# Mean of ReLU over rows of 1024: the order in which 128 partitions take their runs of rows

## The chip, the cores and the metric

The kernel runs on one core of one Trainium2 chip. The metric is the device time of one execution in microseconds (us). Three runs of the kernel before gave a median of 161.53 us (161.38 to 161.6). A difference of about 0.2% (0.3 us) can be told from none.

## The reference

The input `x` is 32 x 512 x 1024 in float32, 67.1 MB. Each output element is the mean of the positive part of one row of 1024:

```python
def reference(x: np.ndarray) -> np.ndarray:
    relu_x = np.maximum(x, 0)
    return np.mean(relu_x, axis=-1).astype(np.float32)
```

So there are 16,384 rows, each is read once, and 64 KB go out. Rows don't depend on each other: any partition may take any rows, as long as its results go back to the right places.

## The kernel before, in words

**Rows and partitions.** The first 128 rows (`xfirst`) go one to each partition, into `row0`. The other 16,256 rows (`xmain`) are cut into 128 runs of J = 127 neighbouring rows; in the kernel before, partition p takes run p. The view `xr` has the indices (partition, row in the run, column), and `outr` is the same for the output.

**Loads.** All of them are issued by the SP engine in program order and go through one queue. `load` (line 109) issues one transfer and gives it a semaphore of its own. There are seven big loads, each of NB = 16 rows of every run, so 64 KB of neighbouring bytes per partition and 8 MB in all, into three buffers that are used in turn. The tail of each run comes in pieces that get smaller: 7, 4, 2 and 1 rows, and the last row in columns 512, 256 and 256 wide. The function `issue_ahead_of_entry_barrier` moves the first two loads (`row0` and the first big one) ahead of the program's entry barrier. Before the load of a buffer that was used before, `buf_free` (line 115) makes SP wait until both compute engines are done with it. Because SP runs ahead as far as the three buffers let it, there are two or more loads in the queue through most of the program.

**Compute.** Rows with an even number in the run are summed on ScalarE (`act_row`, line 15: ReLU with a running sum) and the odd ones on VectorE (`dve_row`, line 20: max with 0, and a sum). Both wait for the load's semaphore. Sums go to `sums`, one column per row of the run. GpSimd (`finish`, line 157) scales them by 1/1024 into `res`. The row before the last is shared between the two engines by columns, and the last row is summed in three parts. The instruction at line 197 does the last part.

**Stores.** The 128 means of `row0` are stored early, between the big loads (line 125). The other 16,256 means are stored by one transfer from `res` (line 205) after the last sum. SP waits for it, and the program ends.

**What sets the order.** Nothing but the order of the instructions on each engine and the semaphores; there is no planner. [...]

Of the kernel before, what the change touches and what calls it, by code (L numbers as in the profile page):

```python
# [45 lines left out]
def kernel(  # L46
# [11 lines left out]
    P = nc.NUM_PARTITIONS  # L58
# [3 lines left out]
    J = R // P  # L62
    inv = 1.0 / D

    xfirst, xmain = xf[:P, :], xf[P:, :]
    outfirst, outmain = out.flatten()[:P], out.flatten()[P:]
    J = J - 1
    xr = xmain.rearrange("(p j) d -> p j d", p=P, j=J)
    outr = outmain.rearrange("(p j) -> p j", p=P, j=J)

    NB = 16
    BUFS = 3
# [7 lines left out]
    def sbuf(name, *shape):  # L80
        return ctx.enter_context(nc.sbuf_tensor(name, list(shape), F32))

    bufs = [sbuf(f"rows{b}", P, NB, D) for b in range(BUFS)]
# [3 lines left out]
    last = sbuf("last", P, D + 2)  # L87
# [20 lines left out]
    def load(i, dst, src):  # L108
        nc.sync.dma_start(out=dst, in_=src).then_inc(loaded[i], 16)

    def buf_free(t):

        if t >= BUFS:
            nc.sync.wait_ge(act, t - BUFS + 1)
            nc.sync.wait_ge(dve, t - BUFS + 1)

    for t in range(full):
        buf_free(t)
        if t == 0:
            load(-1, row0[:, :], xfirst)  # L120
        load(t, bufs[t % BUFS][:, :, :], xr[:, t * NB:(t + 1) * NB, :])
        if t == BUFS:

            nc.sync.wait_ge(first, 2)
            nc.sync.dma_start(
                out=outfirst.rearrange("(q i) -> q i", i=32), in_=turned0[0:P:32, :],
            ).then_inc(stored, 16)
    j0 = full * NB
    buf_free(full)
    xt = bufs[full % BUFS]  # L130
    lo, i = 0, full
    for n in row_pieces:
        load(i, xt[:, lo:lo + n, :], xr[:, j0 + lo:j0 + lo + n, :])
        lo, i = lo + n, i + 1
    c = 0
    for w in col_pieces:
        load(i, last[:, c:c + w], xr[:, J - 1, c:c + w])
        c, i = c + w, i + 1


# [31 lines left out]
    lo, i = 0, full  # L172
    for n in row_pieces[:-1]:
        rows(i, xt, lo, n, j0)
        lo, i = lo + n, i + 1
# [72 lines left out]
```

## Time and profile before

| what | value |
|---|---|
| median of three runs | 161.53 us |
| the profiled execution's own time | 161.59 us |
| its span, first to last instruction | 160.2 us |
| what lies around the span (161.59 - 160.2) | 1.39 us |
| VectorE busy | 73.3 us (46%) |
| ScalarE busy | 70.4 us (44%) |
| DMA packets' time, as a share of 16 engines' span | 97.7% |
| bytes read from HBM | 67.11 MB |
| mean rate over the span | 419 GB/s |

The span starts with the first instruction and ends with the last one. Busy times of different engines overlap. A DMA packet here is what one DMA engine moves in one piece: for a big load, the 64 KB of one partition. SPq in the profile is SP's sequencer, which issues transfers.

### The profile page before, as it was taken

To read this page: it belongs to the slowest core of one execution; us is meant where nothing else is said; L and a number is where in the kernel's file an instruction comes from. 1 tells how busy PE (TensorE), PEld (TensorE's weight loads), DVE (VectorE), ACT (ScalarE), POOL (GpSimd) and SP (SyncE) were. 2 spreads that over 40 slices of the span, in tenths; PEclk is the share of its full clock that TensorE was granted. 3 is DMA by queue.
4 is the path that set the end of the run, shared out by engine and by line. 5 is a ranking of instruction groups with operands and counts; after the bars stand their busy time and mean duration, and the time that the engine had idled before them with its cause. 6 is when DMAs were issued, how large, how long until landed. Compare 5 with 4: busy or idle time off the path is not lost. (4 is left out here: it accounts for less than half of the span.)

```text
span 160.2 us, 347 instructions
## 1 busy us (share of the span) xinstructions
DVE 73.3 (46%) x131; ACT 70.4 (44%) x133; POOL 1.3 (1%) x9
## 2 busy tenths in 40 slices
DVE  0000029900498006960079500993009920299984
ACT  1400029800496006950079300991009900299983
POOL 1000000000000000000000000000000000000001
DMA  9969969979989899699699699699699797998992
GB/s 393 507 278 523 507 278 523 442 344 523 409 376 523 360 425 524 294 491 523 262 524 523 262 523 524 262 523 523 262 524 458 327 523 327 425 451 367 419 412 102
DMA packets 2312, 67.18 MB, mean 419 GB/s; under 512 B 392, under 2 KB 648, under 8 KB 1032
## 3 DMA queue, kind: packets, MB, share of 16 engines
q1 hardware_dynamic: 2312, 67.18, 97.7%
HBM read 67.11 MB, written 0.07 MB: 419 GB/s over the span
## 5 line engine op out<-in xcount | busy, mean ns | idle before, releaser
L20 DVE TENSOR_SCALAR_CACHE_REDUCE rows<-rows 128x1024 f32<-128x1024 f32 (+1 forms) x63 | 72.1, 1208 | 78.9 <-DMA rows<-in_x_dram 78.7
L15 ACT ACTIVATE rows<-rows 128x1024 f32<-128x1024 f32 x64 | 66.2, 1035 | 84.1 <-DMA rows<-in_x_dram 83.9
L15 ACT ACTIVATION_READ_ACCUMULATOR rows<-rows 128x1 f32 x64 | 11.9, 186 | 0.0
L20 DVE DVE_READ_ACCUMULATOR rows<-rows 128x1 f32 x63 | 5.2, 82 | 0.0
L168 DVE STREAM_TRANSPOSE turned<-mean 128x32 f32<-128x32 f32 x1 | 0.2, 213 | 5.9 <-ACT row L164 5.9
L164 ACT ACT_TABLE_LOAD x1 | 1.3, 1283 | 3.3 <-DMA row<-in_x_dram 3.3
L157 POOL TENSOR_SCALAR res<-sums 128x112 f32<-128x112 f32 (+1 forms) x2 | 0.5, 250 | 154.0 <-DVE rows L20 154.0
L164 ACT ACTIVATE row<-row 128x1024 f32<-128x1024 f32 x1 | 1.1, 1056 | 0.0
L15 ACT ACTIVATE last<-last 128x512 f32<-128x512 f32 x1 | 0.6, 630 | 0.0
L20 DVE TENSOR_SCALAR_CACHE_REDUCE last<-last 128x256 f32<-128x256 f32 x1 | 0.4, 420 | 0.3 <-DMA last<-in_x_dram 0.3
L197 DVE SCALAR_TENSOR_TENSOR last<-last,scale 128x258 f32<-128x258 f32 x1 | 0.4, 428 | 0.1
L142 POOL MEMSET scale<- 128x258 f32 x1 | 0.3, 314 | 0.0
L187 POOL TENSOR_SCALAR res<-part 128x1 f32<-128x1 f32 x1 | 0.3, 267 | 0.6 <-DVE rows L20 0.6
L164 ACT ACTIVATION_READ_ACCUMULATOR row<-row 128x1 f32 x1 | 0.2, 186 | 0.0
L15 ACT ACTIVATION_READ_ACCUMULATOR last<-last 128x1 f32 x1 | 0.2, 186 | 0.0
L141 POOL MEMSET mean<- 128x32 f32 x1 | 0.1, 126 | 1.5 <-POOLq L55 1.5
L232 POOL MEMSET const-uint8-127<- 128x1 uint8 x1 | 0.1, 103 | 0.0
L232 POOL MEMSET const-bfloat16-1.0<- 128x1 bf16 x1 | 0.1, 102 | 0.0
L232 POOL MEMSET const-float32-0.0<- 128x1 f32 x1 | 0.1, 99 | 0.2 <-issue 0.2
L232 POOL MEMSET const-float32-1.0<- 128x1 f32 x1 | 0.1, 99 | 0.0
L20 DVE DVE_READ_ACCUMULATOR last<-last 128x1 f32 x1 | 0.1, 83 | 0.0
L197 DVE DVE_READ_ACCUMULATOR last<-last,scale 128x1 f32 x1 | 0.1, 82 | 0.0
## 6 DMA issues: line engine op xcount, KB each, us to landing
rows<-in_x_dram SPq DMA_DIRECT2D x1, 3584.0 KB, 38.1
rows<-in_x_dram SPq DMA_DIRECT2D x1, 2048.0 KB, 42.6
rows<-in_x_dram SPq DMA_DIRECT2D x1, 1024.0 KB, 44.7
row<-in_x_dram SPq DMA_DIRECT2D x1, 512.0 KB, 3.3
rows<-in_x_dram SPq DMA_DIRECT2D x1, 512.0 KB, 45.4
last<-in_x_dram SPq DMA_DIRECT2D x1, 256.0 KB, 45.6
last<-in_x_dram SPq DMA_DIRECT2D x2, 128.0 KB, 45.4
rows<-in_x_dram SPq DMA_DIRECT2D x7, 48.8
```

The lines of the kernel that those rows point to most:

```text
L15: return nc.scalar.activation(out=src, in_=src, func=ACT.Relu, accum_out=acc)
L20: return nc.vector.tensor_scalar(out=src, in0=src, scalar1=0.0, scalar2=init, op0=ALU.max, op1=ALU.add, accum_out=acc,)
L141: nc.gpsimd.memset(mean0[:, :], 0.0)
L142: nc.gpsimd.memset(scale[:, :], inv).then_inc(pool, 1)
L157: nc.gpsimd.tensor_scalar(out=res[:, lo:hi], in0=sums[:, lo:hi], scalar1=inv, scalar2=0.0, op0=ALU.mult, op1=ALU.add,)
L164: nc.scalar.activation(out=row0[:, :], in_=row0[:, :], func=ACT.Relu, scale=inv, accum_out=mean0[:, 0:1],).then_inc(first, 1)
L168: nc.vector.transpose(turned0[:, :], mean0[:, :]).then_inc(first, 1)
L187: nc.gpsimd.tensor_scalar(out=res[:, J - 2:J - 1], in0=part[:, 0:1], scalar1=part[:, 1:2], scalar2=inv, op0=ALU.add, op1=ALU.mult,).then_i ...
L197: nc.vector.scalar_tensor_tensor(out=last[:, 768:], in0=last[:, 768:], scalar=0.0, in1=scale[:, :], op0=ALU.max, op1=ALU.mult, accum_out=r ...
L232: nc = _bacc.Bacc("TRN2", target_bir_lowering=False, num_devices=1)
```

## The change

Run r of 127 rows now goes to another partition. The runs are numbered r = 16 b + e, with b from 0 to 7 and e from 0 to 15, and run r goes to partition p = 8 e + b. So partition 0 has run 0, partition 8 has run 1, partition 16 has run 2, and partition 1 has run 16. Inside a partition nothing changes: 64 KB of neighbouring bytes for each big load, in the same buffer, and the same sums in the same columns. What `x` gives a load is now a view with four indices (e, b, row, column) in place of three, with e outermost; the SBUF side keeps its 128 partitions. The store of `res` uses the same order, so every mean goes to its row. `row0` and its store stay as they are.

```diff
-    xr = xmain.rearrange("(p j) d -> p j d", p=P, j=J)
-    outr = outmain.rearrange("(p j) -> p j", p=P, j=J)
+
+    xr = xmain.rearrange("(b e j) d -> e b j d", e=16, j=J)
+    outr = outmain.rearrange("(b e j) -> e b j", e=16, j=J)
...
-        load(t, bufs[t % BUFS][:, :, :], xr[:, t * NB:(t + 1) * NB, :])
+        load(t, bufs[t % BUFS][:, :, :], xr[:, :, t * NB:(t + 1) * NB, :])
...
-        load(i, xt[:, lo:lo + n, :], xr[:, j0 + lo:j0 + lo + n, :])
+        load(i, xt[:, lo:lo + n, :], xr[:, :, j0 + lo:j0 + lo + n, :])
...
-        load(i, last[:, c:c + w], xr[:, J - 1, c:c + w])
+        load(i, last[:, c:c + w], xr[:, :, J - 1, c:c + w])
```

## The prediction

> **What bounds the kernel now.** I read the page first: busy shares, the row of DMA shares and the queue's total.
>
> ```profile
> span 160.2 us, 347 instructions
> DVE 73.3 (46%) x131; ACT 70.4 (44%) x133; POOL 1.3 (1%) x9
> DMA  9969969979989899699699699699699797998992
> q1 hardware_dynamic: 2312, 67.18, 97.7%
> ```
>
> Compute is idle more than half of the time, while packets fill 97.7% of 16 DMA engines' span. The chain that ended last has only four pieces at the very end, so it doesn't say what made the time. The waits do:
>
> ```profile
> ACT rows L15 <- DMA rows<-in_x_dram: 83.9, 9, 17.2
> DVE rows L20 <- DMA rows<-in_x_dram: 78.7, 8, 16.9
> SPq L115 <- DVE rows L20: 104.6, 5, 29.5
> ```
>
> Both compute engines wait for loads. SP's long wait for buffers (the third line) starves nothing: it runs ahead, and a load lands a median of 48.8 us after its issue, two and a half loads' time, so the queue never empties. Next the timeline: ScalarE's first instruction on each of two neighbouring big loads, and the rate in the stretch between.
>
> ```profile
> 42.32 1.06 ACT L15 ACTIVATE rows<-rows 128x1024 f32<-128x1024 f32 x1 [10.92 <-DMA rows<-in_x_dram]
> 61.69 1.06 ACT L15 ACTIVATE rows<-rows 128x1024 f32<-128x1024 f32 x1 [10.94 <-DMA rows<-in_x_dram]
> 42.30:61.70 19.40, 9.21 (x17) 8.43 (x17) 0.00 (x0) 1.00 1.00 432
> ```
>
> A load of 8.39 MB every 19.37 us is 433 GB/s, or 27.1 GB/s on each of 16 engines; an engine carries 8 partitions' pieces of 64 KB, one after another, at 19.37 / 8 = 2.42 us each. DMA share is 1.00 (the last but one column). So the time is: start of the stream, 127 rows at full rate, and a short tail. The packet records behind the page give the ends: the first 64 KB piece starts 2.75 us into the span, the last piece of the last row ends at 157.4, and the span ends at 160.2. That is 2.75 + 154.6 + 2.8. Around the span lie 161.59 - 160.2 = 1.39 us; the profiled execution is 0.06 us over the median of 161.53.
>
> [...]
>
> **The change, part by part.** *Which engine carries which partition.* This is the part that I think matters. The source is now 16 blocks of 8 runs. If the transfer is divided over 16 engines along the source's outermost index, engine e gets the runs (e, b = 0 to 7), and these belong to partitions 8e to 8e + 7, since the two sides are paired in order. [...] what counts is the moment: all engines start a load with their piece 0[...].
>
> Would they drift apart? In the packet records the 16 first pieces of the first load start within 0.17 us of each other, and the 16 completions of a load arrive within 0.5 us, no wider for the sixth load than for the first. An engine and its partner would have to be four pieces apart, 9.7 us at full rate, to miss each other. [...] The queue isn't drained between loads, and nothing else shifts it. So I take about 0.17 of 9.7 us, 2%, as the part that is not shared, and two engines at half rate for the rest: 4.84 us a piece, about 217 GB/s.
>
> The sum: of the 154.6 us, the pieces down to 2 rows take 152 us: 152 x 1.98 = 301. The last 2.6 us are the 1-row piece and the three column pieces, where four partitions' worth is 0.6 us or less, as small as the leads; I take half of it as shared: 2.6 x 1.5 = 3.9. Data 305, against 154.6. With 2.75 before and 2.8 after: span 310.5; with 1.39 around it, 312 us.
>
> *Issue of the loads.* 14 of the 15 loads get a third dimension in their source. They cost 327 to 462 ns each on SP now; the trace doesn't show a three-dimensional one. Between nothing and a doubling (0.4 us): 13 are hidden behind a queue with two loads in it. The first big load isn't: its data begins 0.4 us or so after `row0`'s ends, so its extra issue time, 0 to 0.4 us, moves everything. I take 0.1, within rounding. Without the cover, 14 x 0.4 would be 5.6 us.
>
> *The store of `res`.* Same 128 packets of 508 B, split in another way: an engine's 4 KB would take 0.15 us at 27.1 GB/s and 0.3 shared. It is on the path; 0 to 0.15 us, taken as 0.1.
>
> *Compute.* Not touched; it is hidden. A load's 16 rows cost 9.2 us on VectorE, against 19.4 us now and some 38 after. `buf_free`'s waits come later by as much as the loads do, and stay behind two queued loads.
>
> *HBM.* Engines side by side now read runs 0.52 MB apart[...] No run here shows it; [...]taken as 0.
>
> **The rivals.**
> - *Leads grow (20%).* [...]the favoured one gains 2.7 GB/s on its partner and is four pieces (256 KB) ahead after some 97 us of sharing; from then on they rarely meet. Data: about 97 us moving 21 MB at 217 GB/s, then 45.6 MB at 433 in 105 us: 202 + 7 = 209 us. With little bias it nears the main case, with strong bias 170. For it: nothing in the trace excludes bias. Against it: leads that never grow now.
> - *Engines keep their partitions[...] (14%).* Then the rate, packets and issues stay, and so does the time: 161.5 us. For it: [...]the pieces have the same sizes. Against it: the pairing argument above.
> - *Only HBM minds (6%).* [...]
> - *Faster (3%).* [...] It decides from a gain of 0.3 us, 0.2% of the stream; against it, there is hardly any room left in DMA share 1.00.
> - The main case has 57%.
>
> **How the numbers follow.** Main case 312 us, own range 295[...] to 320[...]. Range: leaving out unchanged and faster (17%) and 2% above, it goes from 163 to 322, and so takes in the HBM case and growing leads. A difference under 0.2% is what measurement can't tell from none. Faster 0.03; same 0.12 (most of the unchanged case); slower 0.85.
>
> **What would show it.** If the main case is right: 16-row loads become ready every 38 us, not 19.4; GB/s in the middle near 217 while the DMA share stays near 1.0, since packets take twice as long; 2312 packets still; ScalarE's wait before each load about 30 us, not 11. If leads grow: intervals between loads fall from 38 towards 19 us along the run, and completions of one load spread over many us. [...]

## The result, and the profile after

The changed kernel takes 327.34 us (median of six runs, 325.09 to 329.53), against 161.45 us (six runs, 161.24 to 161.6): a ratio of 2.028, with a 95% interval of 2.019 to 2.037. The forecast was 312 us, slower, with a range up to 322. So the direction and the halved rate came as forecast, and the time lies 5 us above the range.

The page of the changed kernel, the same rows as before:

```profile
span 327.2 us, 347 instructions
DVE 73.4 (22%) x131; ACT 70.4 (22%) x133; POOL 1.3 (0%) x9
DMA  9699796996969969699699796996969969699895
q1 hardware_dynamic: 2312, 67.18, 98.8%
```

Same instructions, same 2312 packets and bytes, and the DMA engines look as busy (98.8% of their span): each packet only takes twice as long. The waits say where the time goes:

```profile
ACT rows L15 <- DMA rows<-in_x_dram: 250.0, 11, 38.6
DVE rows L20 <- DMA rows<-in_x_dram: 244.7, 11, 38.2
SPq L116 <- DVE rows L20: 209.2, 5, 49.9
```

ScalarE waits 250.0 us for loads, where it waited 83.9: the difference, 166 us, is nearly the whole loss. The timeline at two neighbouring big loads, and the stretch between them:

```profile
44.44 1.06 ACT L15 ACTIVATE rows<-rows 128x1024 f32<-128x1024 f32 x1 [38.57 <-DMA rows<-in_x_dram]
85.05 1.06 ACT L15 ACTIVATE rows<-rows 128x1024 f32<-128x1024 f32 x1 [32.18 <-DMA rows<-in_x_dram]
44.44:85.05 40.61, 9.21 (x17) 8.43 (x17) 0.00 (x0) 1.00 1.00 207
```

A big load every 40.61 us in place of 19.37, at 207 GB/s with a DMA share of 1.00. By the packet records a piece of 64 KB takes 5.08 us in the mean (median 5.11; 4.95 to 5.13 for those that start after 75 us) in place of 2.42. The stream runs from 2.69 to 323.65 us into the span: 321.0 us where it was 154.6, 166.3 us more before rounding. What follows it grew from 2.87 to 3.59 us, and the start hardly moved (2.69 against 2.75). 166.3 + 0.72 - 0.06 = 167.0 us, the whole difference of the two profiled executions (328.59 - 161.59).

### The profile page after: what moved, and what is told of

Read it like the earlier page. It is cut to its first block, busy times and chain, and to the rows that moved or that the text cites. A ratio compares the mean times of both kernels' runs of the same rounds, so it can differ in the third digit from the quotient of the medians.

```text
span 327.2 us, 347 instructions
## 1 busy us (share of the span) xinstructions
DVE 73.4 (22%) x131; ACT 70.4 (22%) x133; POOL 1.3 (0%) x9
## 2 busy tenths in 40 slices
DMA packets 2312, 67.18 MB, mean 205 GB/s; under 512 B 392, under 2 KB 648, under 8 KB 1032
## 3 DMA queue, kind: packets, MB, share of 16 engines
q1 hardware_dynamic: 2312, 67.18, 98.8%
## 6 DMA issues: line engine op xcount, KB each, us to landing
rows<-in_x_dram SPq DMA_DIRECT2D x1, 2048.0 KB, 98.8
```

## The experiments

Three theories stood at first. A, the forecast's own assumption: the transfer is divided along the source's outermost index, so that each engine has 8 neighbouring partitions, and the 16 engines form eight pairs of partners, which slow each other down while both are in the same half of a load (its first or last four pieces). Partners are "in step" then, and "apart" otherwise. B: runs near each other in memory are slow to read. C: a source with a third dimension is slow in itself. No trace of the kernel before shows pairs, and the records name no engines; A can only be tried by what follows from it.

### The old order of runs, in 16 blocks

```diff
-    xr = xmain.rearrange("(b e j) d -> e b j d", e=16, j=J)
-    outr = outmain.rearrange("(b e j) -> e b j", e=16, j=J)
+    xr = bass.AP(tensor=x.tensor, offset=P * D, ap=[[(8 * J - 1) * D, 16], [J * D, 8], [D, J], [1, D]])
+    outr = outmain.rearrange("(p j) -> p j", p=P, j=J)
```

> Partition p takes run p as in the kernel before, but the source is written as 16 blocks of 8 runs, with each block starting one row early (1015 rows apart, not 1016), so that the two indices don't fold into one; later blocks read rows shifted by up to 15, so the sums are of other rows; bytes and piece sizes are those of before. [...]theory A, that the transfer is divided over the engines by the source's outermost index, so engine e writes partitions 8e to 8e+7[...]: about 325 us, pieces of 64 KB in 5.1 us. Neighbouring runs in memory are slow to read (theory B): here runs that engines read at one time are 4 MB apart, so 161.5 to 165 us and 2.42 us a piece. A source with a third dimension is slow in itself (theory C): about 325 us.

Measured: 325.41 us (2 runs), pieces of 5.00 us in the mean. A stretch in the middle, with the rate in the last column:

```profile
44.00:85.00 41.00, 9.21 (x16) 8.43 (x16) 0.00 (x0) 1.00 1.00 209
```

The interleaving isn't needed for the loss: the old order of runs loses as much, if the source has 16 blocks. B falls here; C doesn't.

### Neighbouring places in memory, with 128 outermost

```diff
-    xr = xmain.rearrange("(p j) d -> p j d", p=P, j=J)
+    xr = bass.AP(tensor=x.tensor, offset=P * D, ap=[[J * D // 4, P], [D, J], [1, D]])
```

> The kernel before, with the runs starting a quarter of a run apart (32,512 elements), [...] the source stays two-dimensional with 128 outermost. The runs overlap and start inside rows, so the sums are of other elements, and only a quarter of the input is read, each part several times; bytes moved and piece sizes are those of before. A: 161.5 us (within 0.5%), 2.42 us a piece. B: well over 200 us, up to about 327. C: 161.5 us.

Measured: 161.8 us (12 runs) against 161.69, a ratio of 1.0006 (0.9993 to 1.0018). Its stretch from 62 to 120 us:

```profile
62.00:120.00 58.00, 27.54 (x49) 25.20 (x49) 0.00 (x0) 1.00 1.00 434
```

434 GB/s, as in the same stretch of the kernel before: runs that start 127 KiB apart in memory (32,512 x 4 B) in place of 508 lose nothing. The prediction's 0 for HBM was right.

### Half of the partitions at a time

```diff
-        nc.sync.dma_start(out=dst, in_=src).then_inc(loaded[i], 16)
+        for h in (slice(0, 64), slice(64, P)):
+            nc.sync.dma_start(out=dst[h], in_=src[h]).then_inc(loaded[i], 16)
...
-        nc.scalar.wait_ge(loaded[i], 16)
-        nc.vector.wait_ge(loaded[i], 16)
+        nc.scalar.wait_ge(loaded[i], 32)
+        nc.vector.wait_ge(loaded[i], 32)
...
```

> The kernel before with each load but row0 issued as two transfers of 64 partitions, 0 to 63 and then 64 to 127; same runs, same piece sizes, two-dimensional sources. A: [...] about twice the stream, 312 us at 4.84 us a piece, 327 us at 5.1. B and C: 161.5 us plus a little for twice as many issues, under 165 us.

Measured: 328.85 us (2 runs), pieces of 5.08 us (median 5.12).

```profile
62.00:120.00 58.00, 9.20 (x16) 8.43 (x16) 0.00 (x0) 1.00 1.05 216
```

(A stretch counts a packet whole where it starts, so its DMA share can pass 1.00 and its rate is too high by as much.) Two-dimensional sources and the old order of runs give the same 5.08 us a piece: loads that go to 64 partitions at a time lose as much as the changed kernel, without a third dimension. That both have one cause, engines in each other's way, is my reading of the equal lengths. The 5% over 4.84 us is also here, so it doesn't need the source in 16 blocks.

### 64 and 32 blocks in place of 16

```diff
-    xr = xmain.rearrange("(b e j) d -> e b j d", e=16, j=J)
-    outr = outmain.rearrange("(b e j) -> e b j", e=16, j=J)
+    xr = xmain.rearrange("(b e j) d -> e b j d", e=64, j=J)
+    outr = outmain.rearrange("(b e j) -> e b j", e=64, j=J)
```

> The changed kernel with e=64 in place of e=16: partition 2e+b takes run 64b+e. [...] A: [...] about 327 us as the changed kernel, 5.1 us a piece; if the 5% over twice 2.42 us is from the reads of neighbouring runs, 4.84 us a piece and 312 us. B: 161.5 to 165 us. C: about 327 us.

Measured: 164.19 us (2 runs), 2.42 us a piece. C falls: the source has its third dimension, and the pieces are as short as before. The plain form of A, that any source with blocks leaves an engine 8 neighbouring partitions, was wrong. The next run has `e=32` in the same two lines.

> The changed kernel with e=32 in place of e=16: partition 4e+b takes run 32b+e, b from 0 to 3. The run with e=64 was fast, so the plain form of theory A, that a third dimension always leaves an engine with neighbouring partitions, has fallen. A2: [...] about 162 to 166 us, 2.42 us a piece. A3: it is kept for 64 alone, for some other reason (the half of 128, say): about 327 us, 5.1 us a piece.

Measured: 164.27 us (2 runs; ratio 1.0146, 1.008 to 1.0211), 2.42 us a piece. Stretches of the runs with 64 and with 32 blocks, in this order:

```profile
62.00:120.00 58.00, 27.62 (x48) 25.28 (x48) 0.00 (x0) 1.00 1.00 434
```

```profile
62.00:120.00 58.00, 27.62 (x48) 25.28 (x48) 0.00 (x0) 1.00 1.00 434
```

So A2 fits, which keeps the rate of before as long as an index of the outermost dimension covers no more than four partitions: with 64 or 32 blocks (two or four partitions) it is 434 GB/s, and with 16 (eight partitions) 207. Which partitions an engine has in each case isn't shown. These two orders do cost about 2.5 us, though. One part of that is seen on SP's timeline: the first three big loads are issued in 4.23 us with 32 blocks, and in 2.29 before.

```profile
0.45 4.23 SPq L110 DMA_DIRECT2D rows<-in_x_dram  x3
```

```profile
0.45 2.29 SPq L109 DMA_DIRECT2D rows<-in_x_dram  x3
```

The longest issue of a big load is 1.70 us with 32 or 64 blocks (0.74 with 16). In the packet records with 32 blocks four engines start the first load at 3.86 to 4.75 us, the others by 2.84, and with 64 blocks the sixteen starts are spread from 2.66 to 4.76. The late ones stay behind until the end: the last piece of the last row ends 1.8 us later than before with 32 blocks, the better part of the 2.4 us. That the longer issues make them late is likely, not shown.

### Is it the moment? A first try, without result

By A the trouble is only that partners are in step. Partners that are four pieces apart should lose nothing. Both the changed kernel and the one before got two extra transfers ahead of the first big load (D in the expectations is the time of one):

```diff
...
+            few = x.flatten_outer_dims().rearrange("(a k) d -> a (k d)", k=4)
+            for parts, n, at in ((12, 512, 0), (4, 512, 512)):
+                nc.sync.dma_start(
+                    out=spare[:parts, at:at + n], in_=few[:parts, 0:2 * n:2], allow_slow_non_contiguous=True,
+                ).then_inc(extra, 16)
...
```

> The changed kernel with two extra transfers between row0 and the first big load: 512 four-byte pieces to each of 12 partitions, and then the same to each of 4, into a spare tensor. [...] A [...]: with D near 9.7 us (four pieces at 2.42) partners miss each other and nearly all pieces take 2.42 us: about 161.5 + 2 x 9.7 = 181 us; with D away from it by x us, a part x/9.7 of each piece is still shared: 161.5 + 2D + 165 x/9.7 us. If the moment doesn't matter (something else about the source in 16 blocks halves the rate): 327 + 2D us and 5.1 us a piece, whatever D.

> The kernel before with the same two extra transfers. A and any other theory: 161.5 + 2D us[...]; 2.42 us a piece. It gives D.

Measured: 337.58 and 178.55 us (one run each). The stagger never came about. SP's timeline of the first (start, length, count):

```profile
0.45 9.04 SPq L126 DMA_DIRECT2D spare<-in_x_dram  x2
9.53 9.70 SPq L112 DMA_DIRECT2D rows<-in_x_dram  x3
```

SP needs 9 us to issue 8,192 pieces of four bytes, and all 16 engines get the first big load behind them, beginning within 0.7 us of each other at 17.5 us. It decides nothing.

### Held back by long pieces, three groups

```diff
...
+            xx = xmain.rearrange("(p j) d -> p j d", p=P, j=J)
+            for n, s in ((4, 70), (4, 69), (4, 67), (12, 39), (12, 2), (12, 36)):
+                at = slice(s, s + 8 * n - 7, 8)
+                nc.sync.dma_start(out=bufs[2][at, :, :], in_=xx[at, :NB, :]).then_inc(extra, 16)
+        if t == 2:
+            nc.sync.wait_ge(extra, 96)
...
```

> The changed kernel with six extra transfers between row0 and the first big load, of pieces of 64 KB into the third buffer before its first use: three to 4 partitions (67, 69 or 70 and every eighth from there) and three to 12 partitions (2, 36 or 39 and every eighth). The earlier try with four-byte pieces kept no engine back by itself: all 16 engines began the first big load within 0.7 us, at 17.5 us, so it says nothing. These transfers are few and long, so the first big load is issued behind them within 2 to 3 us[...]. [...] Theory A [...]: after the first load, big loads land about 21.6 us apart in place of 40.6, most pieces take 2.42 us, total about 205 us (190 to 220). If the rate is halved whatever the moment: 40.6 us apart, 5.1 us a piece, about 350 us.

> The kernel before with the same six extra transfers, to see what they cost: both theories: big loads 19.4 us apart after the first, 2.42 us a piece after the first load[...]: some 195 us.

Measured: the changed kernel so, with the six extra transfers issued in 4.36 us, 307.95 us in the profiled run (317.88 in another), the kernel before so 197.57 us (2 runs). The second is as expected. The first isn't: big loads still come some 34.9 us apart.

```profile
68.48 1.06 ACT L15 ACTIVATE rows<-rows 128x1024 f32<-128x1024 f32 x1 [59.05 <-DMA rows<-in_x_dram]
103.41 1.06 ACT L15 ACTIVATE rows<-rows 128x1024 f32<-128x1024 f32 x1 [26.50 <-DMA rows<-in_x_dram]
138.19 1.06 ACT L15 ACTIVATE rows<-rows 128x1024 f32<-128x1024 f32 x1 [26.35 <-DMA rows<-in_x_dram]
```

The completions of the first big load fall into three groups: four engines at 48.7 to 49.0 us, eight at 59.2 to 59.7, four at 68.3 to 68.5. I take the last as engines with six extra pieces each, the middle as those with three, the first as those with none. A piece starts within 0.03 us of the end of the same engine's piece before it, so the pieces can be strung into 16 chains, and these agree with it: four have 62 pieces of 64 KB, eight 59 and four 56, where a kernel without extra pieces has 56 in each. By the starts and lengths of their pieces, neighbouring groups are 2.65 and 2.2 pieces apart. I take the four held back most as partners of four of the eight, and the other four of the eight as partners of those not held back; so there are two sets of four pairs. If partners in step slowed only each other, pieces would take 2.42 us for 2.2 or 2.65 of every four, and loads would be near 29 us apart, as an estimate from these lengths (8 x (0.55 x 2.42 + 0.45 x 5.11) for the pairs that are 2.2 of four apart). What the stretches show is another thing; the rate is the last column:

```profile
50.70:65.30 14.60, 0.00 (x0) 0.00 (x0) 0.00 (x0) 1.00 0.91 211
65.30:67.80 2.50, 0.00 (x0) 0.00 (x0) 0.00 (x0) 1.00 1.22 341
67.80:75.60 7.80, 7.11 (x13) 7.12 (x13) 0.00 (x0) 1.00 0.86 185
75.60:82.80 7.20, 2.09 (x4) 1.31 (x4) 0.00 (x0) 1.00 1.06 255
82.80:85.30 2.50, 0.00 (x0) 0.00 (x0) 0.00 (x0) 1.00 1.06 315
```

(A short stretch is blurred, as packets count where they start.) The only stretches above 300 GB/s are the two of 2.5 us, in which both sets of pairs are apart. In 67.8 to 75.6 only the last group and half of the middle one are in step; but the first group, apart from its partners, has pieces of 4.94 to 5.02 us there. Partners in step seem to hold up everybody. That was theory A+: one pair in step is enough to slow all 16 engines. The next two runs were made for it.

### Both sets of pairs apart, and one set apart

By the same assumption, the pairs are in two sets, and extra transfers to 4 partitions hold back only one side of one set. To bring both sets apart, the extra transfers of the run before are changed to these; for one set, only the five of 4 partitions are kept:

```diff
-            for n, s in ((4, 70), (4, 69), (4, 67), (12, 39), (12, 2), (12, 36)):
-                at = slice(s, s + 8 * n - 7, 8)
+            for n, s in ((4, 36), (4, 37), (4, 38), (4, 0), (4, 1), (12, 4), (12, 5), (12, 6), (12, 7), (12, 8)):
+                at = slice(s, s + 9 * n - 8, 9)
...
-            nc.sync.wait_ge(extra, 96)
+            nc.sync.wait_ge(extra, 160)
```

> As the run with six held-back transfers, but with five to 4 partitions (from 36, 37, 38, 0 and 1) and five to 12 partitions (from 4 to 8), every ninth partition[...]. What the six-transfer run showed: engines in three groups 2.2 and 2.65 pieces apart, and every engine slow[...]; all fast only in the stretch in which both pairs were apart. Theory A+ ([...]nothing else is wrong with the source in 16 blocks): worked out with that rule, big loads land about 22 us apart (21 to 26), nearly all pieces 2.42 us, total about 230 us (220 to 255), of which some 45 us are the extra pieces. A without the hold-up of others: about 37 us apart after the first few, as each engine drifts by itself. If the moment doesn't matter: 40.6 us apart and over 350 us.

> The changed kernel with only the five extra transfers to 4 partitions (from 36, 37, 38, 0 and 1, every ninth). [...] A+ [...]: all pieces stay at 5.1 us, big loads complete on 12 engines 40.9 us apart and on four engines some 18 us later each; total 335 to 350 us. A without the hold-up: [...] some 40% of the pieces before 80 us take under 3 us; total about 325 us[...].

Measured: 255.96 us (2 runs) with both sets apart, 338.65 us (2 runs) with one. Both sets apart, three neighbouring stretches from load to load:

```profile
76.21:100.49 24.28, 9.21 (x16) 8.42 (x16) 0.00 (x0) 1.00 0.97 348
100.49:125.06 24.57, 9.20 (x16) 8.42 (x16) 0.00 (x0) 1.00 1.02 363
125.06:149.00 23.94, 9.21 (x16) 8.42 (x16) 0.00 (x0) 1.00 0.99 359
```

One set apart, the same kind of stretch:

```profile
71.57:111.73 40.16, 9.21 (x16) 8.42 (x16) 0.00 (x0) 1.00 1.00 209
```

The changed kernel's own loads, with its own order of runs and 16 blocks, run at 348 to 363 GB/s once partners are mostly out of step, and half of their pieces take what they took before (the table below): nothing else is wrong with them. With 80 extra pieces to move at the start it is still 71 us faster than the changed kernel without them. And with only one set out of step (four engines complete each big load 14 to 20 us after the last of the others), nothing is gained. The lengths of 64 KB pieces that start after 75 us, from the packet records:

```
                          pieces   mean us   under 2.6 us   over 4.6 us
before                       416      2.43            99%            0%
changed kernel               656      5.08             0%          100%
one set apart                688      5.02             0%          100%
three groups                 700      4.35             0%           56%
both sets apart              687      3.01            53%            4%
```

With one set apart, not one of these 688 pieces is faster than 4.7 us, although by the assumed pairs half of the engines are apart from their partners by then. A+ expected 335 to 350 us for it; the rival expected 325 us and two fifths of the pieces before 80 us fast, and 2 of 243 take under 3 us. So all 16 engines stay slow while four pairs are still in step, as A+ has it.

A+ as it was worded, one pair for all, goes too far, and the run with both sets apart shows it. Strung into chains, its pieces leave a time, from 88.4 to 92.2 us, in which, by the assumed pairs, just one engine is in step with its partner:

```profile
88.40:92.20 3.80, 0.00 (x0) 0.00 (x0) 0.00 (x0) 1.00 0.92 397
```

The two pieces of that pair take 4.32 and 4.09 us; the nine pieces of other engines that start and end in this time take 2.43 to 2.49. The same pair meets from 75.1 to 78.8 and from 101.9 to 105.5 us, with much the same result (its longest pieces 4.77 and 4.39 us, those of others inside 2.6 to 3.0 and 2.5 to 2.6). The four engines that were held back most are in the same half together from 88.4 to 92.2 us, at full rate, so they aren't partners of one another; the reading of the run with one set apart rests on that. So, by the assumed pairs, one pair in step slows its own two engines (4.09 and 4.32 us), and with four pairs in step all 16 are slow (4.7 to 5.1 us); what two or three do was not worked out.

The 230 us of A+ for both sets apart was too low (256, just past its range of 220 to 255): loads were 24, not 22 us apart, and the seventh came after 36 us. From about there the engines are at different sizes of pieces at one moment, so that their distances no longer fit; that last is argued, not tested.

## Why the prediction was right or wrong

- *Which engine carries which partition*: not shown; the records name no engines, so the partitions of each stay an assumption. The loss that it was to explain is there: 16 blocks lose what 128 partitions outermost had, shown from both sides: the loss without the interleaving (16 blocks in the old order, 325.41 us), and nearly none with an interleaving of 32 or 64 blocks (164.27 and 164.19 us), for which the plain form of A had given a loss too.
- *Two engines at half rate while they are in step*: right in its effect, by the half transfers (5.08 us a piece) and by the run with both sets apart (53% of the pieces under 2.6 us). What the engines get in each other's way at was not shown.
- *4.84 us a piece at half rate*: this is the term that was mis-sized, and why the time left the range. A piece takes 5.11 us. With all eight pairs in step, a pair moves 2 x 65,536 B in 5.11 us, 25.6 GB/s, where one engine of the kernel before moves 27.1; why stays open. The piece is 5.6% longer than 4.84, and the own range, up to 320 us, left 8 us for this. On the big loads that is 40.6 us and not the 38.3 that the sum has (8 x 2.42 x 1.98), 7 x 2.3 = 16 us in all, as much as the data part missed (321.0 against 305).
- *The 2% taken off for leads*: wrong as a step. Pairs that are apart gain nothing while four others are in step (no piece under 4.7 us with one set apart). In the changed kernel it mattered little, as leads were small: the mean piece of 5.08 against 5.11 is 0.6%, not 2%.
- *Half of the last 2.6 us shared*: the sum's 3.9 us came out near (from the end of the last 2-row piece, 319.45 us, to that of the last column piece, 323.65, are 4.2 us; between their completions 3.9), but by luck. "Half shared" would make every one of these pieces 1.5 times as long; those of one row took 0.29 us in place of 0.16, 1.84 times as long, and only those of the last two column pieces 1.5 times.
- *Issue of the loads*: an issue grew from a median of 0.335 to 0.567 us; the first load's data began no later (2.69 us). The 0.1 us taken was nothing; the bound of 0.4 held for the start.
- *The store of `res`*: mis-sized. The time after the stream grew by 0.72 us, where 0.1 was taken and 0.15 was the bound. Of it 0.64 lie between the start of the store's issue and the end of the span; the issue itself went from 0.35 to 0.58 us. The estimate had counted the data and forgotten the issue of a store with a third dimension (with 16 blocks in the load alone, the store's issue still took 0.35 us); the other 0.4 us are not explained.

```profile
158.57 0.35 SPq L205 DMA_DIRECT2D out_dram<-res  x1
```

```profile
324.93 0.58 SPq L206 DMA_DIRECT2D out_dram<-res  x1
```

- *Rivals*: leads did not grow by themselves: load after load, the sixteen completions of the changed kernel keep the same 0.7 to 0.8 us between first and last. A gain or a loss by reads of neighbouring runs had no part in it (1.0006 with runs 127 KiB apart).

## What to carry to other kernels

Look at the outermost dimension of a load's source before reordering it: here 16 kept all 16 DMA engines busy (a DMA share of 1.00), but at 207 GB/s, where 32, 64 and 128 gave 434. The sign in a profile is a DMA share near 1.0 with half of the GB/s, and the packets' lengths doubled (2.42 to 5.08 us) with their sizes unchanged; that DMA engines are busy doesn't mean that they move data at full rate. With 32 or 64 blocks neighbouring runs lie 4 or 2 partitions apart in place of 8, for about 1.5% of the time; but as reads from neighbouring places gained nothing here (1.0006), there was no reason to want it.

## What the runs showed of the hardware that I had not expected

DMA engines can be slow with no partner in step, by the assumed pairs, while other pairs are in step. With one of two sets of pairs four pieces apart and the other in step, all 688 pieces stay at 4.7 to 5.1 us; with both apart, 53% take 2.42 to 2.6 us. It takes more than one pair in step: while a single pair met, its pieces took up to 4.8 us and those of other engines 2.4 to 3.0. Whether the writes, the reads or something else ties the engines together stays open; no run here separates them. So does why two engines in step move less together (25.6 GB/s) than one alone (27.1).
